# Half of a retention output projection as seven products on stored sums, and norms from a tile of ones

## The chip, the cores and the metric

The kernel runs on 1 core of one Trainium2 chip. The metric is the device time of one execution in microseconds (us), taken as the median of several runs. TensorE (PE in the profile) multiplies matrices, VectorE (DVE) and ScalarE (ACT) work element by element, GpSimd (POOL) and SyncE (SP) here mostly issue transfers (DMA) between the chip's DRAM and its on-chip memory. Every engine works through its own instructions in their written order; semaphores hold an instruction until what it needs is there.

## The reference, cut to what matters

The program is a two-layer encoder on 1024 tokens with 1024 features: forgetting attention, then a gated FFN, then retention, then a second gated FFN, with RMS norms between. The change lies in the retention layer:

```python
def retention(h, w_in, w_out):
    ...
    # per head (4 heads, value width 512), over chunks of 64 tokens:
    a = einsum(q, k) * d_intra;  inner = a @ v
    cross = (q @ state) * q_decay
    state = state * chunk_decay + (k * k_decay).T @ v
    y = inner + cross
    ...
    mu = jnp.mean(y, axis=-1, keepdims=True)
    var = jnp.mean(jnp.square(y - mu), axis=-1, keepdims=True)
    y = ((y - mu) * lax.rsqrt(var + EPS)).reshape(B, S, H * dv)
    return (jax.nn.silu(g) * y) @ w_out        # w_out: 2048 x 1024
```

So each head's output is normed for each token over 512 values, multiplied by its gate, and the four heads' 2048 features go through one projection to 1024.

## The kernel before

Features stand on the 128 partitions, tokens along the rows (two halves of 512). All products are made in float32 precision from two parts: `split` writes hi with ScalarE (a rounded copy) and lo = source - hi with VectorE, and a product is three matmuls, hi x hi, hi x lo and lo x hi. The instructions of each engine are put in order by a scheduler when the program is built; the pools (`bpa` with 32 buffers of 128x512, `bpb` with 24, `y`, `st` with 5 of 128x1024, `wp` for split weights) decide when a buffer may be written again.

The large projections, in the FFN among others, use seven products for a 2x2 block product in place of eight (`Products`, L672–L674): the operands are seven sums of the four blocks of each factor, named A11, S1, S2, A12, S3, A22, S4 on the side of the weights (made by `Blocks`) and B11, T1, T2, B21, T3, T4, B22 on the other (`Stored` or `Combos`). The output projection of the retention does not: it has 16 feature tiles and is done in two halves of 8, `mm_u` (L110–L112) with eight tiles of weights from `wtile2`. The first half adds the old residual (L1254), the second is `out_proj`.

The retention runs in eight stages (head h, token half ib). A stage makes the next stage's `scores` and weighs the values with its own (`weighted`, L1178–L1180; `crossed` with the state carried over, L1189–L1191), then calls `finish`, which evacuates the four outputs, sums their squares in `acc` (the mean has been taken off the values in `load_v`), and takes the norm: `colsum` (L165) multiplies the sums with a column of ones, so that tokens stand on partitions; `rsqrt` works on 128x4 values with ScalarE's square root; `rows` (L173) spreads the result over all partitions again. The tiles times this factor (for head 0 also times the gate g) are stored to `zd`. After the second half of a head, `prepare` loads the next head's k, q (`load_parts`, from `kd` and `qd`, in hi and lo parts) and v, and `state` makes its state. Behind the last stage `load_units` reads `zd` back, multiplies by the gates `gd` (for heads 1 to 3) and splits. All of these transfers stand in SP's one queue.

## Time and profile before

| | us |
|---|---|
| median of 3 runs | 2582.19 (2580.89 to 2583.51) |
| the profiled execution | 2582.71 |
| its span, first to last instruction | 2580.8 |
| PE, DVE, ACT, POOL busy in it | 2557.4, 1833.6, 1242.7, 210.1 |
| retention stages with their norms, about | 1583 to 1758 |
| first half of the output projection, about | 1758 to 1841 |
| second half, about | 1841 to 1927 |

A row of instructions gives the line, engine, operation, output <- inputs by the program's names and the shape, then busy time and mean length of one. A matmul's printed length overlaps the next one; what one costs is read from start to start. A wait is put down to what was released last.

### The profile page before, as it was taken

Reading aid. Unit: us, or ns where it says so; the run is one execution under the profiler, and the core shown is the slowest. Engines: PE = TensorE matmul, PEld = TensorE weight load, DVE = VectorE, ACT = ScalarE, POOL = GpSimd, SP = SyncE. Lnnn points to the kernel's source line nnn. Section 1 sums busy time; section 2 is a strip of 40 time slices with the busy share of each in tenths; the row PEclk is TensorE's granted clock in tenths of the full one; section 3 lists DMA queues with packets and bytes.
Section 4 is the critical chain, followed back from the end, with each engine's and each line's share of the span. In section 5 each row is a group of like instructions: output and inputs, shape, how many; then the busy total and the mean of one; then the engine's idle time right before and its main releaser. Section 6 shows DMA issues by size and latency. Waiting matters only on the chain.

```text
span 2580.8 us, 35315 instructions
## 1 busy us (share of the span) xinstructions
PE 2557.4 (99%) x12756; PEld 2177.7 (84%) x12756; DVE 1833.6 (71%) x3107; ACT 1242.7 (48%) x2331; POOL 210.1 (8%) x205
## 2 busy tenths in 40 slices
PE   9999999999999999999999999999999999999998
PEld 8889887888888887889898988988888888888888
DVE  6798888976666768886666576775668666668694
ACT  6566656643333455454444436552355333335543
POOL 0143323000000001001111110000000000000200
PEclk9999999999999999999999999999999999999999
DMA  3111142432332344533343335765522323225541
GB/s 131 45 58 59 57 147 85 157 110 95 114 106 94 124 162 155 182 112 115 121 141 123 127 135 191 254 220 191 205 101 87 106 98 110 101 84 192 169 150 66
DMA packets 148655, 327.86 MB, mean 127 GB/s; under 512 B 17280, under 2 KB 30592, under 8 KB 148480
## 3 DMA queue, kind: packets, MB, share of 16 engines
q1 hardware_dynamic: 143280, 310.38, 35.4%
q0 software_dynamic: 4480, 14.68, 1.7%
q8 instruction: 100, 1.64, 0.3%
q14 instruction: 75, 0.61, 0.1%
q10 hardware_dynamic: 720, 0.55, 0.1%
HBM read 225.40 MB, written 100.14 MB: 126 GB/s over the span
## 4 chain that ended last, share of the span: by engine, by line
PE 94%; DVE 2%; DMA 2%; issue 1%; ACT 1%; POOL 0%; SPq 0%; DVEq 0%; POOLq 0%; ACTq 0%
PE mm L672 18%; PE mm L673 18%; PE mm L674 18%; PE mm L110 7%; PE mm L111 7%; PE mm L112 7%; PE mm L792 2%; PE mm L790 2%; PE mm L791 2%; PE mm L279 1%; PE mm L278 1%; PE mm L277 1%; PE mm L1178 1%; PE mm L1180 1%; PE mm L1179 1%
## 5 line engine op out<-in xcount | busy, mean ns | idle before, releaser
L673 PE MATMUL mm<-b,wh 128*128 128x512 f32 x2128 | 827.9, 389 | 1.2 <-DVE b L103 1.2
L672 PE MATMUL mm<-b,wh 128*128 128x512 f32 x2128 | 825.7, 390 | 1.6 <-DVE 22_4485_22699 L732 0.8
L674 PE MATMUL mm<-b,wl 128*128 128x512 f32 x2128 | 824.3, 389 | 0.0
L102 ACT CAST wh<-st 128x512 fp32r<-128x512 f32 (+4 forms) x450 | 275.9, 615 | 496.1 <-PE mm L673 320.3
L672 PEld LDWEIGHTS mm<-b,wh 128*128 128x128 f32 x2128 | 399.5, 188 | 85.6 <-DVE 22_4485_22699 L732 1.2
L673 PEld LDWEIGHTS mm<-b,wh 128*128 128x128 f32 x2128 | 399.6, 188 | 83.6 <-DVE b L103 1.6
L674 PEld LDWEIGHTS mm<-b,wl 128*128 128x128 f32 x2128 | 399.5, 188 | 83.3 <-DVE wl L103 0.3
L103 DVE TENSOR_TENSOR wl<-st,wh 128x512 fp32r<-128x512 f32 (+4 forms) x450 | 310.6, 695 | 181.0 <-ACT wh L102 176.1
L102 ACT CAST wh<-s 128x512 fp32r<-128x512 f32 x252 | 156.4, 622 | 294.5 <-PE mm L673 256.0
L110 PE MATMUL mm<-b,wh 128*128 128x512 f32 x736 | 286.3, 393 | 7.2 <-ACT b L130 4.9
L111 PE MATMUL mm<-b,wh 128*128 128x512 f32 x736 | 287.4, 391 | 1.7 <-DVE b L103 1.7
L112 PE MATMUL mm<-b,wl 128*128 128x512 f32 x736 | 287.0, 391 | 0.0
L103 DVE TENSOR_TENSOR wl<-s,wh 128x512 fp32r<-128x512 f32 x252 | 180.3, 717 | 103.7 <-ACT wh L102 99.6
L110 PEld LDWEIGHTS mm<-b,wh 128*128 128x128 f32 x736 | 138.7, 188 | 36.6 <-ACT b L130 5.2
L111 PEld LDWEIGHTS mm<-b,wh 128*128 128x128 f32 x736 | 138.8, 189 | 29.5 <-DVE b L103 2.2
L112 PEld LDWEIGHTS mm<-b,wl 128*128 128x128 f32 x736 | 138.6, 188 | 28.6
L520 POOL DMA_DIRECT2D b<-ac_B x24 | 13.4, 559 | 1399.4 <-PE mm L673 1396.9
L791 PE MATMUL mm<-wl,b 128*128 128x256 f32 x448 | 126.4, 283 | 0.0
L790 PE MATMUL mm<-wh,b 128*128 128x256 f32 x448 | 126.2, 283 | 0.0
L792 PE MATMUL mm<-wh,b 128*128 128x256 f32 x448 | 126.0, 283 | 0.0
L624 DVE TENSOR_TENSOR s<-st 128x512 f32<-128x512 f32 x84 | 58.0, 691 | 74.3 <-DMA st<-ffn_in 35.3
L102 ACT CAST b<-st 128x512 fp32r<-128x512 f32 (+1 forms) x136 | 77.8, 606 | 53.3 <-DVE st L828 18.9
(527 smaller groups left out, 4118.8 us busy)
## 6 DMA issues: line engine op xcount, KB each, us to landing
st<-ffn_in SPq DMA_DIRECT2D x88, 512.0 KB, 3.6
st<-ffn_out_pairs SPq DMA_DIRECT2D x32, 512.0 KB, 4.1
ac_T<-t SPq DMA_DIRECT2D x48, 256.0 KB, 2.3
xo<-xd SPq DMA_DIRECT2D x32, 256.0 KB, 2.9
ac_B<-t SPq DMA_DIRECT2D x32, 256.0 KB, 2.4
st<-ac_T SPq DMA_DIRECT2D x16, 512.0 KB, 4.4
b<-ac_T POOLq DMA_DIRECT2D x32, 256.0 KB, 5.7
st<-ret_qk SPq DMA_DIRECT2D x16, 512.0 KB, 3.9
```

Of the source, the lines that this page charges most:

```text
L102: nc.scalar.copy(hi, src)
L103: return nc.vector.tensor_tensor(lo, src, hi.bitcast(F32), op=ALU.subtract)
L110: nc.tensor.matmul(ps, wh, xh, start=(first and k == 0), stop=False, skip_group_check=free)
L111: nc.tensor.matmul(ps, wh, xl, start=False, stop=False, skip_group_check=free)
L112: nc.tensor.matmul(ps, wl, xh, start=False, stop=(last and k == n - 1), skip_group_check=free)
L624: nc.vector.tensor_tensor(self.s1, self.a21, self.a22, op=ALU.add)
L672: nc.tensor.matmul(ps, hi[:, js], th, start=first and j == 0, stop=False, skip_group_check=True)
L673: nc.tensor.matmul(ps, hi[:, js], tl, start=False, stop=False, skip_group_check=True)
L674: nc.tensor.matmul(ps, lo[:, js], th, start=False, stop=(j == 3), skip_group_check=True)
L790: nc.tensor.matmul(o, th[:, tk], hi[:, js], start=f, stop=False, skip_group_check=True)
L791: nc.tensor.matmul(o, th[:, tk], lo[:, js], start=False, stop=False, skip_group_check=True)
L792: nc.tensor.matmul(o, tl[:, tk], hi[:, js], start=False, stop=(j == 3), skip_group_check=True)
```

## The change

1. **Seven products.** The feature tiles 0 to 7 (heads 0 and 1) of the output projection go through `Products` in four blocks of two output tiles. The weights' pieces are read from `ret_o` as 128x4x128 (`Blocks` with `rows`). The other side is a `Stored` object zc with the pools of MAP4. `finish` multiplies the gates in for heads 0 and 1, stores the first token half as B11 and B21, and after the second half reads these back (e0, o0), makes T1, T2, T3, T4 with four VectorE instructions per pair of tiles and stores them and B22. `zc.get` loads and splits them again by POOL's queue, during stages 5, 6 and 7. The tiles 8 to 15 are loaded by the new `Acts`, two at a time, during the last block of products.
2. **Norms.** `finish` splits `acc` and multiplies it with a 128x128 tile of ones (L1256, L1258), which gives the sum on every partition at once; a third matmul (L1257) adds the row of eps, scaled to fit, that lies in two rows of the tile ez and is loaded before each finish from `ed`. Ln and Exp on ScalarE and three VectorE instructions, all 512 wide, make the factor.
3. **One function table.** With Ln and Exp in place of the square root, one table is loaded ahead; kap, rho and the states are rescaled (`passed`) so that the sums of the norm keep in range.
4. **Queues.** The part loads of kd and qd are issued by POOL and not by SP.

The line numbers of the changed kernel are higher: L672–L674 become L693–L695, L103 becomes L106, L828 becomes L849. The orders below are the written orders of one engine, line, operation, output <- inputs, shape; names with numbers are buffers.

TensorE's work around the norm of one stage (head 1, first half) before the change, where cs and rw are the norm's two results among the matmuls of scores and state:

```order
L1152 MATMUL mm_16415<-b_16296,b_16254 128x384
L1153 MATMUL mm_16415<-b_16297,b_16254 128x384
L1154 MATMUL mm_16415<-b_16296,b_16255 128x384
L1152 MATMUL mm_16415<-b_16300,b_16258 128x384
L165 MATMUL cs_16221<-ones,yacc_16202 128x1 x4
L1153 MATMUL mm_16415<-b_16301,b_16258 128x384
L1154 MATMUL mm_16415<-b_16300,b_16259 128x384
```

and at the same norm now, with sm the sum, ah and al its split input:

```order
L1223 MATMUL mm_16401<-wh_16217,b_15871 128x256
L1256 MATMUL sm_16261<-ah_16257,ones 128x512
L1257 MATMUL sm_16261<-ez,ones 128x512
L1167 MATMUL mm_16615<-b_16352,b_16317 128x512
L1168 MATMUL mm_16615<-b_16353,b_16317 128x512
L1169 MATMUL mm_16615<-b_16352,b_16318 128x512
L1167 MATMUL mm_16615<-b_16358,b_16317 128x512
L1258 MATMUL sm_16261<-al_16258,ones 128x512
L1168 MATMUL mm_16615<-b_16359,b_16317 128x512
```

The column sums, and the later spread of rows with them, are replaced by three full-width matmuls, between other work as before.

VectorE in the finish of head 1's second half, now: fb is the norm's factor, g the gates, e and o (numbers 3224, 3225 and 3228, 3229) the first halves read back, t the sums:

```order
L1272 TENSOR_TENSOR yt_16536<-yt_16536,g_16570 128x512
L1272 TENSOR_TENSOR yt_16539<-yt_16539,g_16574 128x512
L1272 TENSOR_TENSOR yt_16544<-yt_16544,g_16578 128x512
L1272 TENSOR_TENSOR yt_16549<-yt_16549,g_16582 128x512
L1283 TENSOR_TENSOR t_3226_16587<-yt_16536,e_3224_16585 128x512
L1284 TENSOR_TENSOR t_3227_16588<-yt_16539,t_3226_16587 128x512
L1285 TENSOR_TENSOR yt_16536<-yt_16539,yt_16536 128x512
L1286 TENSOR_TENSOR o_3225_16586<-o_3225_16586,t_3227_16588 128x512
L1283 TENSOR_TENSOR t_3230_16602<-yt_16544,e_3228_16600 128x512
L1284 TENSOR_TENSOR t_3231_16603<-yt_16549,t_3230_16602 128x512
L1285 TENSOR_TENSOR yt_16544<-yt_16549,yt_16544 128x512
L1286 TENSOR_TENSOR o_3229_16601<-o_3229_16601,t_3231_16603 128x512
```

Before, only four multiplications by the factor stood here. Sixteen instructions are now in a row, ahead of the next norm's sums (yacc) and its split.

SP's queue at the same place, now, where zcB and zcT are the stored operands:

```order
L1282 DMA e_3224_16585<-zcB_15389 128x512
L1282 DMA o_3225_16586<-zcB_15393 128x512
L632 DMA st_17787<-ret_o 128x4x128
L1288 DMA zcB_15394<-yt_16539 128x512
L1288 DMA zcB_15394<-yt_16549 128x512
L1288 DMA zcT_15391<-t_3226_16587 128x512
L1282 DMA e_3228_16600<-zcB_15389 128x512
L1288 DMA zcT_15390<-t_3227_16588 128x512
L1288 DMA zcT_15392<-yt_16536 128x512
L1282 DMA o_3229_16601<-zcB_15393 128x512
L1288 DMA zcT_15395<-o_3225_16586 128x512
L1288 DMA zcT_15391<-t_3230_16602 128x512
```

The second pair's e (3228) is loaded behind the store of the first pair's t (3226), and its o (3229) behind two more stores.

The diff, without the lines that only rescale:

```diff
--- before.py
+++ after.py
...
@@ -527,6 +530,20 @@
     MAP2 = dict(zip(NAMES, (bpa, bpa, bpa, bpa, bpb, bpb, bpb)))
     MAP3 = dict(zip(NAMES, (bpa, bpa, bpa, bpb, bpb, bpb, bpa)))
 
+    MAP4 = dict(zip(NAMES, (bpa, bpa, bpb, bpb, bpb, bpa, bpa)))
+    ACTS = {"A11": (6, 7), "S1": (0, 1), "A12": (2, 3), "S3": (4, 5)}
+
+    class Acts:
+
+
+        def __init__(self, srcs):
+            self.srcs, self.t = srcs, {}
+
+        def get(self, i):
+            if i not in self.t:
+                self.t[i] = load_units(bpb if i < 6 else bpa, *self.srcs[i])
+            return self.t[i]
+
     class Combos:
         def __init__(self, gi, pools):
             self.gi, self.pools = gi, pools
@@ -605,12 +622,16 @@
     class Blocks:
 
 
-        def __init__(self, src):
+        def __init__(self, src, rows=False):
             self.s1, self.ready = None, {}
             sts = []
             for i in range(2):
                 st = sp.tile([P, 1024], F32, tag="st", name=nm("st"), bufs=5)
-                nc.sync.dma_start(st, src[:, i * 1024:(i + 1) * 1024])
+                if rows:
+                    for t in range(2):
+                        nc.sync.dma_start(st[:, HALF[t]].rearrange("p (j c) -> p j c", j=4), src[i][:, t])
+                else:
+                    nc.sync.dma_start(st, src[:, i * 1024:(i + 1) * 1024])
                 sts.append(st)
             self.a11, self.a12 = sts[0][:, 0:512], sts[0][:, 512:1024]
             self.a21, self.a22 = sts[1][:, 0:512], sts[1][:, 512:1024]
@@ -1056,11 +1077,30 @@
     nc.vector.tensor_tensor(r2, rc, rc, op=ALU.mult)
     kap = small([P, RET_HEADS, TB], "kap", 1)
     rho = small([P, RET_HEADS, TB], "rho", 1)
-    rho2 = small([P, RET_HEADS, TB], "rho2", 1)
+
...
+    ps = mp.tile([P, H], F32, tag="ms", name=nm("tr"))
+    n = RET_HEADS * TB
+    nc.tensor.transpose(ps[:n, :P], rho.rearrange("p h b -> p (h b)"), ident)
+    er = [yr("er")[:n, :P] for _ in range(2)]
+    nc.scalar.activation(er[0], ps[:n, :P], AF.Copy, scale=512 * EPS)
+    nc.vector.scalar_tensor_tensor(er[1], ps[:n, :P], 512 * EPS, er[0].bitcast(F32), op0=ALU.mult, op1=ALU.subtract)
+    ed = dp.tile([2, RET_HEADS * S], F32, tag="ed", name="ed")
+    for i, t in enumerate(er):
+        nc.gpsimd.dma_start(ed[i].rearrange("(n p) -> n p", p=P), t.bitcast(F32))
+    ez = sp.tile([P, H], F32R, tag="xo", name="ez", bufs=2)
+    nc.scalar.activation(ez, R[:, :H], AF.Copy, scale=0.0)
...
@@ -1081,7 +1121,7 @@
             for e in range(2):
                 r[e][i] = units(bpa)
                 for t, part in zip(r[e][i], src[e]):
-                    nc.sync.dma_start(t.bitcast(F32), part[:, HALF[i]])
+                    nc.gpsimd.dma_start(t.bitcast(F32), part[:, HALF[i]])
         return r
 
     def load_k(h):
@@ -1115,7 +1155,7 @@
             kt += [(hi[:, b * 256:(b + 1) * 256], lo[:, b * 256:(b + 1) * 256]) for b in range(2)]
         return ks, kt
 
-    def state(kt, vv):
+    def state(h, kt, vv):
 
         r = []
         for e in range(2):
@@ -1127,7 +1167,10 @@
                 nc.tensor.matmul(ps, kh[:, es], vh, start=(b == 0), stop=False)
                 nc.tensor.matmul(ps, kh[:, es], vl, start=False, stop=False)
                 nc.tensor.matmul(ps, kl[:, es], vh, start=False, stop=(b == 3))
-            r.append(bsplit(bpa, ps))
+            hi, lo = units(bpa)
+            nc.scalar.activation(hi, ps, AF.Copy, scale=passed[h])
+            nc.vector.scalar_tensor_tensor(lo, ps, passed[h], hi.bitcast(F32), op0=ALU.mult, op1=ALU.subtract)
+            r.append((hi, lo))
         return r
 
     zero = cp.tile([P, P], F32, tag="tri", name="zero")
@@ -1191,11 +1234,15 @@
                 nc.tensor.matmul(yps[vt], sl[:, vs], qh, start=False, stop=False)
 
     def finish(h, ib, yps):
+        nc.gpsimd.dma_start(ez.bitcast(F32)[:2, :], ed[:, h * S + ib * H:h * S + (ib + 1) * H])
         acc = sp.tile([P, H], F32, tag="sacc", name=nm("yacc"), bufs=2)
         ys = []
         for vt in range(4):
             y = yu("yt")
-            nc.scalar.copy(y, yps[vt])
+            cp_ = nc.scalar.copy(y, yps[vt])
+            if vt == h == ib == 0:
+                with tc.issue_after(cp_.ins):
+                    nc.scalar.preload_act_table_set("natural_log_exp_and_others")
             if vt == 0:
                 nc.scalar.activation(acc, y, AF.Square)
             else:
@@ -1203,24 +1250,47 @@
                 nc.scalar.activation(sq, y, AF.Square)
                 nc.vector.tensor_tensor(acc, acc, sq, op=ALU.add)
             ys.append(y)
-        cs = colsum(acc, mp, "ms")
-        var = small([P, 4], "yv")
-        rs = slice(4 * ib, 4 * ib + 4)
-        nc.vector.scalar_tensor_tensor(var, cs[:, 0:4], 1.0 / 512, rho2[:, h, rs], op0=ALU.mult, op1=ALU.mult)
-        r = rsqrt(var, 1.0, 4)
-        fac = small([P, 4], "yf")
-        nc.vector.tensor_tensor(fac, r, rho[:, h, rs], op=ALU.mult)
-        fb = rows(fac, mp, "ms")
+        hi, lo = yr("ah"), yr("al")
+        split(hi, lo, acc)
+        ps = mp.tile([P, H], F32, tag="ms", name=nm("sm"))
+        nc.tensor.matmul(ps, onesr, hi, start=True, stop=False)
+        nc.tensor.matmul(ps, onesr, ez, start=False, stop=False)
+        nc.tensor.matmul(ps, onesr, lo, start=False, stop=True)
+        q, fb = yu("q"), yu("fb")
+        nc.scalar.activation(q, ps, AF.Ln, scale=1.0 / 512)
+        nc.scalar.activation(q, q, AF.Exp, scale=-0.5)
+        nc.vector.scalar_tensor_tensor(fb, ps, -0.5 / 512, q, op0=ALU.mult, op1=ALU.mult)
+        nc.vector.tensor_tensor(fb, fb, q, op=ALU.mult)
+        nc.vector.scalar_tensor_tensor(fb, fb, 1.5, q, op0=ALU.add, op1=ALU.mult)
         for vt in range(4):
             nc.vector.tensor_tensor(ys[vt], ys[vt], fb, op=ALU.mult)
-            if h < 1:
-                g = yu("g")
-                nc.sync.dma_start(g, gd[4 * h + vt][:, HALF[ib]])
-                nc.vector.tensor_tensor(ys[vt], ys[vt], g, op=ALU.mult)
-            nc.sync.dma_start(zd[4 * h + vt][:, HALF[ib]], ys[vt])
-
+            if h > 1:
+                nc.sync.dma_start(zd[4 * h + vt][:, HALF[ib]], ys[vt])
+                continue
+            g = yu("g")
+            nc.sync.dma_start(g, gd[4 * h + vt][:, HALF[ib]])
+            nc.vector.tensor_tensor(ys[vt], ys[vt], g, op=ALU.mult)
+            if ib == 0:
+                j = 2 * h + vt // 2
+                nc.sync.dma_start(zc.d[("B11", "B21")[vt % 2]][:, j * H:(j + 1) * H], ys[vt])
+        if h < 2 and ib == 1:
+            for j in (2 * h, 2 * h + 1):
+                js = slice(j * H, (j + 1) * H)
+                e1, o1 = ys[j % 2 * 2:j % 2 * 2 + 2]
+                e0, o0, t1, t2 = yu("e0"), yu("o0"), yu("t1"), yu("t2")
+                for t, n in ((e0, "B11"), (o0, "B21")):
+                    nc.sync.dma_start(t, zc.d[n][:, js])
+                nc.vector.tensor_tensor(t1, e1, e0, op=ALU.subtract)
+                nc.vector.tensor_tensor(t2, o1, t1, op=ALU.subtract)
+                nc.vector.tensor_tensor(e1, o1, e1, op=ALU.subtract)
+                nc.vector.tensor_tensor(o0, o0, t2, op=ALU.subtract)
+                for n, t in (("T1", t1), ("B22", o1), ("T2", t2), ("T3", e1), ("T4", o0)):
+                    nc.sync.dma_start(zc.d[n][:, js], t)
+
+
+    zc = Stored("zc", MAP4, False)
     prepare(0)
-    heads[0][4] = state(heads[0][1], heads[0][3])
+    heads[0][4] = state(0, heads[0][1], heads[0][3])
     stages = [(h, ib) for h in range(RET_HEADS) for ib in range(2)]
     a = [scores(0, 0, dg) for dg in range(4)]
     for i, (h, ib) in enumerate(stages):
@@ -1230,6 +1300,9 @@
         yps = [mm_ps() for _ in range(4)]
         if ib == 1:
             crossed(h, yps)
+        if i == 7:
+            zc.get("T4")
+            zc.get("B22")
         an = []
         for dg in range(4):
             if nxt:
@@ -1238,21 +1311,40 @@
         a = an
         finish(h, ib, yps)
         if ib == 1 and nxt:
-            heads[h + 1][4] = state(heads[h + 1][1], heads[h + 1][3])
-
-    zg = list(zip(zd, [None] * (4 * 1) + gd[4 * 1:]))
+            heads[h + 1][4] = state(h + 1, heads[h + 1][1], heads[h + 1][3])
+        for n in {5: ("B11", "T1"), 6: ("T2", "B21"), 7: ("T3",)}.get(i, ()):
+            zc.get(n)
+
+
     y = [[None, None] for _ in range(KT)]
-    acts = [load_units(bpa, *t) for t in zg[:8]]
-    for n in range(KT):
-        w = wtile2(d["ret_o"][n], 8)
-        for h in range(2):
-            ps = mm_ps()
-            mm_u(ps, w, acts, h)
-            y[n][h] = yu("y")
-            xo = sp.tile([P, H], F32, tag="xo", name=nm("xo"), bufs=2)
-            nc.sync.dma_start(xo, xd2[n][:, HALF[h]])
-            nc.vector.tensor_tensor(y[n][h], ps, xo, op=ALU.add)
-    X, nrm, nw = out_proj(d["ret_o"], y, [load_units(bpb if i < 6 else bpa, *t) for i, t in enumerate(zg[8:])], xd, 3, d["ffn_in"][1, 0], MAP3)
+    acts = Acts(list(zip(zd[8:], gd[8:])))
+    banks[0] += 1
+
+    def blocks(n):
+        w = [d["ret_o"][2 * n + i][:, :D].rearrange("p (j t c) -> p t j c", t=2, c=P) for i in range(2)]
+        return Blocks(w, True)
+
+    prod = Products(blocks(0), zc).open()
+    for n in range(KT // 2):
+        u = {q: yu(q) for q in ("11", "12", "21", "22")}
+
+        def closed(b, c):
+            nc.scalar.copy(u["22"], b)
+            nc.vector.tensor_tensor(u["22"], c, u["22"], op=ALU.add)
+
+        prod.middle(lambda b: nc.scalar.copy(u["12"], b), closed)
+        nxt = Products(blocks(n + 1), zc, (acts, ACTS) if n == 2 else None).open() if n < 3 else None
+        prod.close()
+        nc.vector.tensor_tensor(u["12"], prod.c, u["12"], op=ALU.add)
+        for i in range(2):
+            for h in range(2):
+                t = u[f"{i + 1}{h + 1}"]
+                xo = sp.tile([P, H], F32, tag="xo", name=nm("xo"), bufs=2)
+                nc.sync.dma_start(xo, xd2[2 * n + i][:, HALF[h]])
+                nc.vector.tensor_tensor(t, ((prod.a, t), (prod.b, t))[i][h], xo, op=ALU.add)
+                y[2 * n + i][h] = t
+        prod = nxt
+    X, nrm, nw = out_proj(d["ret_o"], y, [acts.get(i) for i in range(8)], xd, 3, d["ffn_in"][1, 0], MAP3)
     ffn(1, X, nrm, xd, None, True, nw, MAP3)
 
 
```

More of the change, by code (lines that the diff above doesn't have):

```diff
@@ L78, in yu, with yr @@
         return yp.tile([P, H], F32, tag="y", name=nm(s))
+    def yr(s):
+        return yp.tile([P, H], F32R, tag="y", name=nm(s))
     def units(pool):
```

12 lines of the change are left out of this document (9 added, 3 removed).

## The prediction

> **What bounds the kernel now.** I read the page's busy shares first, then its chain of waits, then the stretch that the change touches, by windows.
>
> ```profile
> span 2580.8 us, 35315 instructions
> PE 2557.4 (99%) x12756; PEld 2177.7 (84%) x12756; DVE 1833.6 (71%) x3107; ACT 1242.7 (48%) x2331; POOL 210.1 (8%) x205
> PE 94%; DVE 2%; DMA 2%; issue 1%; ACT 1%; POOL 0%; SPq 0%; DVEq 0%; POOLq 0%; ACTq 0%
> ```
>
> TensorE (PE) is busy in 99% of the span and is 94% of the chain that ended last. So time is saved by taking TensorE instructions away, and lost where another engine then makes TensorE wait. The retention with its norms lies at about 1583–1758 us, the first half of the output projection at 1758–1841 us.
>
> ```profile
> 1600.00:1650.00 50.00, 49.27 (x277) 43.29 (x276) 37.60 (x86) 31.57 (x69) 0.00 (x0) 1.00 0.77 248
> 1650.00:1700.00 50.00, 50.00 (x316) 46.09 (x315) 37.84 (x96) 29.33 (x66) 0.00 (x0) 1.00 0.78 254
> 1700.00:1758.00 58.00, 57.51 (x329) 51.36 (x328) 42.03 (x93) 34.09 (x73) 0.00 (x0) 1.00 0.65 212
> ...
> PE mm L1178 <- ACT wh L1167: 0.7, 1, 0.7
> PE mm L1152 <- DMA b<-qd30h: 0.3, 1, 0.3
> ```
>
> The columns of the first rows are the stretch, its length, then the busy time of PE, PE's weight loads, DVE, ACT and POOL, the granted clock (1.00), the DMA share and GB/s. PE has no gap here; the waits (1583–1945 us) show its two longest, 1.0 us together. But DVE (VectorE) is busy for 117.5 of these 158 us, 74%, and the DMA engines for 65–78%. There is some room for new work there, and not much.
>
> **What the change takes from TensorE.** These rows give the pace of a 128x512 matmul and the two norm steps that go.
>
> ```profile
> 1629.70 0.39 PE L1178 MATMUL mm<-wh,b 128*128 128x512 f32 x1
> 1629.93 0.39 PE L1179 MATMUL mm<-wl,b 128*128 128x512 f32 x1
> 1630.16 0.95 PE L165 MATMUL cs<-ones,yacc 128*128 128x1 f32 x8
> 1630.97 0.49 PE L1180 MATMUL mm<-wh,b 128*128 128x512 f32 x1
> 1631.29 0.34 PE L1178 MATMUL mm<-wh,b 128*128 128x384 f32 x1
> 1631.47 0.33 PE L1179 MATMUL mm<-wl,b 128*128 128x384 f32 x1
> ...
> 1636.68 0.28 PE L1180 MATMUL mm<-wh,b 128*128 128x256 f32 x1
> 1636.80 1.05 PE L173 MATMUL rw<-ident,yf 128*128 128x128 f32 x8
> 1637.61 0.36 PE L1178 MATMUL mm<-wh,b 128*128 128x256 f32 x1
> 1637.81 0.28 PE L1179 MATMUL mm<-wl,b 128*128 128x256 f32 x1
> ...
> L173 PE MATMUL rw<-ident,yf 128*128 128x128 f32 x64 | 8.4, 274 | 0.0
> L165 PE MATMUL cs<-ones,yacc 128*128 128x1 f32 x64 | 7.6, 239 | 0.0
> ```
>
> From start to start, 128x512 costs 0.227 us, 128x384 0.18, 128x256 0.12. The printed 0.39 us overlaps the next and is not what one costs.
>
> 1. Products. Before, feature tiles 0–7 take 8 output tiles x 2 halves x 8 tiles x 3 matmuls = 384. After, 4 blocks x 7 products x 4 x 3 = 336, of the same shape. 48 x 0.227 = **-10.9 us**.
> 2. Norms. The column sums start at 1630.16 and the next matmul at 1630.97: 0.81 us, and that next one takes 0.32 instead of 0.227. The rows start at 1636.80 and end at 1637.61: 0.81, and the next takes 0.20 instead of 0.12. Together 1.79 us; the grouped rows have 64 records of each, 8 a finish, so eight finishes: **-14.3 us**.
> 3. In their place come 3 matmuls of 128x512 a finish: 24 x 0.227 = **+5.4 us**. One 128x128 transpose is added, costed as one of the four steps of L173 (0.81/4): **+0.2 us**.
>
> Sum on TensorE: **-19.6 us**. The profiled execution took 2582.71 us (its span and 1.9 us around it), 0.5 above the median of 2582.19, so with everything hidden the time would be 2563.1 us. The four function-table loads that go are ACT work beside a busy PE and count for nothing.
>
> **What comes back: VectorE.** What leaves TensorE lands on DVE: splits of the sums that come back from DRAM, five 512-wide steps and a split for each norm, the gates of head 1, 16 sums and differences. Its pace, again start to start:
>
> ```profile
> 1607.78 0.68 DVE L103 TENSOR_TENSOR b<-mm,b 128x512 fp32r<-128x512 f32 x1
> 1608.38 0.34 DVE L1163 SCALAR_TENSOR_TENSOR atd<-mm,kap,mask 128x128 f32<-128x128 f32 x1
> 1608.64 0.74 DVE L1074 SCALAR_TENSOR_TENSOR b<-st,vmean,b 128x512 fp32r<-128x512 f32 x1
> 1609.30 0.29 DVE L103 TENSOR_TENSOR wl<-atd,wh 128x128 fp32r<-128x128 f32 x1
> 1609.50 0.35 DVE L1163 SCALAR_TENSOR_TENSOR atd<-mm,kap,mask 128x128 f32<-128x128 f32 x1
> 1609.76 0.61 DVE L1168 SCALAR_TENSOR_TENSOR wl<-mm,kap,wh 128x384 fp32r<-128x384 f32 x1
> 1610.28 0.28 DVE L103 TENSOR_TENSOR wl<-atd,wh 128x128 fp32r<-128x128 f32 x1
> 1610.48 0.48 DVE L1168 SCALAR_TENSOR_TENSOR wl<-mm,kap,wh 128x256 fp32r<-128x256 f32 x1
> 1610.88 0.29 DVE L103 TENSOR_TENSOR wl<-atd,wh 128x128 fp32r<-128x128 f32 x1
> ```
>
> So 512 wide costs 0.60 us (0.66 with vmean), 384 wide 0.52, 256 wide 0.40, 128 wide 0.20 to 0.26. I counted the changed order on both engines between the same two events: the split that feeds the ones-matmul of the second finish (head 0, second half) and that of the last one (head 3, second half). DVE has 159 instructions 512 wide (11 with vmean), 4 of 384, 13 of 256 and 48 of 128: 95.4 + 0.7 + 2.1 + 5.2 + 11.0 = 114.4 us. PE has 320, 84 and 175 matmuls of 512, 384 and 256, and 16 transposes at 0.2: 72.6 + 15.1 + 21.0 + 3.2 = 111.9 us. In the last part, between the last two finishes, it is 19.9 us of DVE against 12.0 of PE, since the weight sums and splits of the first product blocks stand there. DVE has no slack left, and **2.5 us** are short even if it never stands still.
>
> It will stand still. DVE works in written order, and in finish the second pair's e0 is loaded only after the store of the first pair's t1 on the in-order SP queue (the orders of VectorE and of SP in the section on the change). From the end of t1, three more instructions (1.8 us) cover that load. Its landing time:
>
> ```profile
> zd<-yt SPq DMA_DIRECT2D x32, 256.0 KB, 2.9
> g<-gd SPq DMA_DIRECT2D x8, 256.0 KB, 4.9
> st<-gd SPq DMA_DIRECT2D x12, 512.0 KB, 4.7
> b<-ac_T POOLq DMA_DIRECT2D x32, 256.0 KB, 5.7
> ```
>
> A 256 KB transfer lands in 2.9 us (stores) to 4.9 us (loads of gates): 1.1 to 3.1 us uncovered, middle 2.1, once per head. Behind a standing DVE are the next scores' splits and the next acc sums, for which PE waits. Two heads: **4.2 us**. The stand-stills that DVE has today (below) I take as mostly filled by the longer queue; bounds of the whole DVE term 0 (its 74% today left TensorE only 1.0 us of waits) to 25 us (third rival), value **6.7 us**, nearer the low end because the count is of work and not of waits.
>
> **What comes back: transfers.** Operands now fill the pools until the last block, so all 16 loads of 512 KB for tiles 8–15 go through five st buffers in its time. Each tile holds two buffers for a landing (4.7 us), a 1024-wide multiply (twice 0.60) and two splits on ACT and DVE, some 8.5 us; two and a half tiles are in flight, so 3.4 us a tile and 27 us for eight. From the last finish to the projection's second half the written order has some 214 matmuls of 128x512, 48 us of cover; if the loads start late it is about half of that. Bounds 0 and 5 us, value **2 us**. The 48 loads of kd and qd move from SP to POOL: landing there is 5.7 us against 4.9 for SP's g, and the cover is most of a head's matmuls, so nothing; if that cover is gone, each of three heads pays the 0.8 us of difference.
>
> The nearest thing that the trace has to the new 28 reloads is the FFN's change of group, where as many are split within some 20 us:
>
> ```profile
> PE mm L673 <- DVE b L103: 1.2, 1, 1.2
> PE mm L672 <- DVE 22_1856_9302 L732: 0.8, 1, 0.8
> ...
> 989.82 1.90 POOL L520 DMA_DIRECT2D b<-ac_B  x3 [0.16 <-issue]
> ```
>
> There TensorE lost 2.0 us (975–1005 us). Here they are spread over three stages, which is why I add nothing for them beyond the DVE count.
>
> The Trainium skill, page "SBUF — State Buffer", section "SBUF: two separate sides", speaks against moving loads to POOL: transfers issued there need descriptors that GpSimd writes, and it is locked out while VectorE holds their shared ports in a two-port mode. The last row has three issues in 1.90 us, 0.63 each, beside a DVE that was splitting; no run here yet shows these loads beside a DVE with no gaps.
>
> **Sum:** 2582.7 - 19.6 + 6.7 + 2.0 = 2571.8, so **2572 us**.
>
> **Rivals.**
>
> *All hidden*, 2563 us: for it speaks today's 1.0 us of waits; against it the 114.4 us of DVE work beside 111.9. Chance 0.16.
>
> *The reloads of e0 and o0 in a crowd*, no change: with the DMA share at 0.78 already and some 8 MB more in the stretch (28 reloads, 8 reads of e0 and o0 and 12 more stores of 256 KB, less 8 loads of 512 KB), the landing doubles from 4.9 to 9.8 us; DVE then stands 9.8 - 1.8 = 8 us per head, 16 for both. 2582.7 - 19.6 + 2.5 + 16 + 2 = 2584 us. It decides from 4.7 us a head, where the sum passes 2577. Chance 0.22.
>
> *POOL issues wait out DVE*, no change: were each of the 16 part loads of a head held for one 0.60 us instruction, the last would be 9.6 us later; exposed at one head it makes 2582 us. The row of three issues in 1.90 us speaks against. The skill's rule above would be its cause. Chance 0.04.
>
> *DVE keeps its stand-stills*, slower. Its waits at 1583–1760 us:
>
> ```profile
> DVE yv L1209 <- PE cs L165: 9.6, 4, 4.8
> DVE b L1074 <- ACT b L1073: 9.4, 11, 1.7
> DVE wl L103 <- ACT wh L102: 4.9, 9, 2.1
> DVE b L103 <- ACT b L102: 4.7, 4, 2.0
> ```
>
> They make 28.6 us in 177, so 18 in 111.9. The same turn from TensorE to ScalarE to VectorE remains in each norm. With no slack, each of them is TensorE's wait: DVE costs 2.5 + 4.2 + 18 = 25 us, the time is 2582.7 - 19.6 + 25 + 2 = 2590 us. It decides once 15.6 of the 18 us remain, where the sum passes 2587.4. Against it: an engine with a full queue finds its inputs ready more often. Chance 0.18.
>
> That the products cost more than 0.227 us a matmul, so that the change saves less, I leave out: their form, a 128x128 weight tile against a moving 128x512, is that of the rows L1178 and L1179 above, and of what they replace.
>
> **Chances and range.** A measurement of this kernel tells about 0.2%, 5.2 us, from no change: faster is below 2577.0, slower above 2587.4. My forecast, with 2566–2577 as its own range, has 0.40; with all hidden, faster has 0.56. The crowd and POOL give 0.26 for the same, stand-stills 0.18 for slower. Below 2562 only a PE that also loses its old waits would come, above 2589 about half of the slow case: range 2562 to 2589.
>
> **What would show it.** In the changed profile: L693–L695 at 0.227 us; no L165 or L173 in the retention; PE idle of some 9 us in place of 1.0, most of it released by DVE between the sixth finish and the second product block; DVE over 90% busy there; DVE's t1 of the second pair waiting for a DMA by 1–3 us; the last block's waits for DMA or its splits below 5 us. I am wrong if PE's waits in the retention stay under 3 us (all hidden), or if DVE's waits for e0 exceed 7 us, for ACT 16 us, or for PE the share of them that L1209 has now.

## The result, and the profile after

| | before | changed |
|---|---|---|
| median, us | 2581.89 (5 runs, 2579.03 to 2583.51) | 2606.08 (5 runs, 2602.89 to 2611.77) |
| profiled execution, us | 2582.71 | 2603.95 |
| its span, us | 2580.8 | 2601.5 |

The changed kernel is slower: 1.0097 of the time before (95% interval 1.0083 to 1.0111). The forecast was 2572 us with a range of 2562 to 2589.

The page of the changed kernel, with the rows that answer to the first three of the prediction:

```profile
span 2601.5 us, 35255 instructions
PE 2552.2 (98%) x12605; PEld 2165.8 (83%) x12605; DVE 1884.7 (72%) x3161; ACT 1269.4 (49%) x2381; POOL 255.1 (10%) x291
PE 90%; DVE 3%; DMA 3%; issue 2%; ACT 1%; POOL 0%; SPq 0%; DVEq 0%; POOLq 0%
```

PE is busy for 5 us less, not 20, in a span that is 21 us longer, and its share of the chain fell from 94% to 90%. (The work of 19.6 us did go; the slow clock described below puts some 14 us of longer matmuls in its place.) The windows over the changed stretch (stretch, length, PE busy, PE's weight loads, DVE, ACT, POOL, granted clock, DMA share, GB/s) show two things:

```profile
1583.00:1640.00 57.00, 56.49 (x303) 48.94 (x302) 39.01 (x79) 38.47 (x77) 15.25 (x28) 1.00 0.70 225
1640.00:1700.00 60.00, 53.07 (x275) 46.17 (x274) 45.92 (x94) 28.75 (x65) 9.64 (x18) 0.94 0.80 275
1700.00:1760.00 60.00, 48.71 (x233) 41.12 (x232) 44.69 (x92) 30.77 (x69) 13.01 (x25) 0.86 0.65 222
1760.00:1800.00 40.00, 36.11 (x169) 30.34 (x168) 39.20 (x67) 28.40 (x54) 8.52 (x16) 0.96 0.63 211
1800.00:1850.00 50.00, 49.03 (x215) 40.01 (x215) 37.84 (x57) 19.94 (x35) 0.00 (x0) 1.00 0.59 207
1850.00:1900.00 50.00, 46.45 (x202) 37.49 (x201) 34.30 (x53) 21.41 (x37) 0.00 (x0) 1.00 0.61 206
```

First, PE stands: length less busy time is 27.1 us here, and 1.2 us in the same stretch before. Second, its clock was not always granted: one less the clock, times the length, is 3.6 + 8.4 + 1.6 = 13.6 us. With the prediction's sum for the work alone, 2563.1 + 25.9 + 13.6 = 2602.6 us, against 2603.95 of this execution. The prediction added 8.7 us for what comes back (6.7 for VectorE, 2.0 for the transfers of the last block); these two numbers make 39.5. The whole miss lies in them.

Where PE stood (its waits, sum, times and longest), and the matmuls behind the first long stop:

```profile
PE sm L1256 <- ACT ah L105: 10.2, 2, 5.3
PE mm L1232 <- ACT yt L1242: 4.0, 1, 4.0
PE mm L693 <- ACT yt L1242: 3.9, 1, 3.9
...
1679.53 0.79 PE L1256 MATMUL sm<-ah,ones 128*128 128x512 f32 x1 [5.32 <-ACT ah L105]
...
1680.55 0.63 PE L1167 MATMUL mm<-b,b 128*128 128x512 f32 x1
1680.98 0.63 PE L1168 MATMUL mm<-b,b 128*128 128x512 f32 x1
1681.40 0.63 PE L1169 MATMUL mm<-b,b 128*128 128x512 f32 x1
```

Four stops of 3.9 to 5.3 us carry 18 us. Behind the first, a 128x512 matmul takes 0.425 us from start to start in place of 0.227, for about 7 us. VectorE's own waits and the landings (KB each, us from issue to landing) say who was late:

```profile
DVE yt L1272 <- DMA g<-gd: 14.0, 5, 6.4
DVE t L1283 <- DMA e<-zcB: 7.5, 3, 3.3
...
g<-gd SPq DMA_DIRECT2D x16, 256.0 KB, 8.6
e<-zcB SPq DMA_DIRECT2D x4, 256.0 KB, 6.1
```

The second long stop, at head 1, shows the chain in the timeline (start, length, engine, instruction, in brackets the idle time before it and what ended it):

```profile
1703.43 5.12 SPq L632 DMA_DIRECT2D st<-ret_o  x7
1708.60 6.54 SPq L1271 DMA_DIRECT2D g<-gd  x4
...
1705.19 0.56 POOL L1124 DMA_DIRECT2D b<-qd30h  x1
...
1711.04 0.54 POOL L1124 DMA_DIRECT2D b<-qd31l  x1 [1.74 <-DMA b<-qd30h]
...
1720.18 2.69 DVE L1272 TENSOR_TENSOR yt<-yt,g 128x512 f32<-128x512 f32 x4 [6.37 <-DMA g<-gd]
...
1720.91 1.32 ACT L1242 COPY yt<-mm 128x512 f32<-128x512 f32 x2 [9.39 <-DVE yt L1272]
...
1721.54 0.79 PE L1232 MATMUL mm<-b,b 128*128 128x512 f32 x1 [4.04 <-ACT yt L1242]
```

SP's loads of weights and gates and POOL's loads of qd run at once. The gates are asked for late and land late: in the whole kernel SP's issue of one gate load takes up to 3.1 us (0.8 in E1 below, where POOL issues no part loads). VectorE stands 6.4 us; ScalarE's copy of the next outputs waits for tiles that VectorE holds, 9.4 us; and PE waits for the bank of its result memory that this copy empties.

The last of the four stops, ahead of the first block of products, is of another kind. VectorE is busy for 39.2 of the 40 us from 1760 us on, among the splits of the reloaded sums. ScalarE, in its own order, waits for reloads that have not landed, and the copy of the outputs that PE needs stands behind their splits:

```profile
ACT b L105 <- DMA b<-zcT: 5.2, 3, 2.8
...
1788.13 0.80 PE L693 MATMUL mm<-b,wh 128*128 128x512 f32 x1 [3.89 <-ACT yt L1242]
```

### The profile page after: what moved, and what is told of

It is laid out like the page before. It is cut to its first block, busy times and chain, and to the rows that moved or that the text cites. A ratio compares the mean times of both kernels' runs of the same rounds, so it can differ in the third digit from the quotient of the medians.

```text
span 2601.5 us, 35255 instructions
## 1 busy us (share of the span) xinstructions
PE 2552.2 (98%) x12605; PEld 2165.8 (83%) x12605; DVE 1884.7 (72%) x3161; ACT 1269.4 (49%) x2381; POOL 255.1 (10%) x291
## 4 chain that ended last, share of the span: by engine, by line
PE 90%; DVE 3%; DMA 3%; issue 2%; ACT 1%; POOL 0%; SPq 0%; DVEq 0%; POOLq 0%
PE mm L693 19%; PE mm L694 19%; PE mm L695 19%; PE mm L113 6%; PE mm L114 6%; PE mm L115 6%; PE mm L813 2%; PE mm L811 2%; PE mm L812 2%; PE mm L280 1%; PE mm L282 1%; PE mm L281 1%; DMA g<-gd 1%; DMA e<-zcB 1%; DMA st<-gd 1%
## 5 line engine op out<-in xcount | busy, mean ns | idle before, releaser
L693 PE MATMUL mm<-b,wh 128*128 128x512 f32 x2240 | 869.9, 390 | 7.7 <-ACT yt L1242 3.9
L695 PE MATMUL mm<-b,wl 128*128 128x512 f32 x2240 | 868.7, 389 | 0.0
L693 PEld LDWEIGHTS mm<-b,wh 128*128 128x128 f32 x2240 | 420.9, 188 | 97.5 <-ACT yt L1242 4.3
L695 PEld LDWEIGHTS mm<-b,wl 128*128 128x128 f32 x2240 | 420.9, 188 | 87.7
L106 DVE TENSOR_TENSOR wl<-st,wh 128x512 fp32r<-128x512 f32 (+4 forms) x450 | 310.8, 695 | 171.5 <-ACT wh L105 167.3
L105 ACT CAST wh<-s 128x512 fp32r<-128x512 f32 x264 | 163.8, 622 | 308.3 <-PE mm L694 271.8
L106 DVE TENSOR_TENSOR wl<-s,wh 128x512 fp32r<-128x512 f32 x264 | 188.5, 716 | 104.2 <-ACT wh L105 100.0
L114 PEld LDWEIGHTS mm<-b,wh 128*128 128x128 f32 x608 | 114.8, 189 | 24.6 <-DVE b L106 2.2
L115 PEld LDWEIGHTS mm<-b,wl 128*128 128x128 f32 x608 | 114.5, 188 | 23.4
L105 ACT CAST b<-st 128x512 fp32r<-128x512 f32 (+1 forms) x120 | 69.0, 605 | 49.8 <-DMA st<-ac_T 16.0
```

What stands on the lines that cost most here:

```text
L105: nc.scalar.copy(hi, src)
L106: return nc.vector.tensor_tensor(lo, src, hi.bitcast(F32), op=ALU.subtract)
L114: nc.tensor.matmul(ps, wh, xl, start=False, stop=False, skip_group_check=free)
L115: nc.tensor.matmul(ps, wl, xh, start=False, stop=(last and k == n - 1), skip_group_check=free)
L693: nc.tensor.matmul(ps, hi[:, js], th, start=first and j == 0, stop=False, skip_group_check=True)
L695: nc.tensor.matmul(ps, lo[:, js], th, start=False, stop=(j == 3), skip_group_check=True)
```

## The experiments

E1 is the base of several others, since it has one part less of the change. Each ratio is to the kernel before on the same chip, with its 95% interval.

**E1, the queue.** The part loads on SP again:

```diff
-                    nc.gpsimd.dma_start(t.bitcast(F32), part[:, HALF[i]])
+                    nc.sync.dma_start(t.bitcast(F32), part[:, HALF[i]])
```

> The changed kernel with the 48 part loads of kd and qd issued by SP again, as before; nothing else. In the changed kernel VectorE stood 14.0 us for gates that landed in 8.6 us (4.9 before) and TensorE had four stops of 4 to 5.3 us. Theory 'crowd by POOL': the part loads now run beside the gate loads and slow them; on SP the gates land in about 5 us again, VectorE's wait for them falls below 5 us, and the time falls by 10 to 25 us, to 2580-2596 us. Rival 'the gates and read-backs are late by their own place': behind 16 more loads in SP's order they come no earlier; 2600-2625 us.

2602.5 us, 1.0081 (1.0066 to 1.0096): 3.6 us less than the change, with runs that overlap (2601.1 to 2603.9 against 2602.9 to 2611.8). The gates landed in 5.7 us and VectorE no longer waited for them, as 'crowd' said, but the time did not follow; it lies in the range of the rival. The wait moved to the read-backs:

```profile
1710.57 0.69 DVE L1284 TENSOR_TENSOR t<-yt,t 128x512 f32<-128x512 f32 x1
...
1713.85 0.32 SPq L1282 DMA_DIRECT2D e<-zcB  x1
...
1721.09 0.69 DVE L1283 TENSOR_TENSOR t<-yt,e 128x512 f32<-128x512 f32 x1 [8.63 <-DMA e<-zcB]
...
1718.40 0.59 ACT L1242 COPY yt<-mm 128x512 f32<-128x512 f32 x1 [7.13 <-DMA zcB<-yt]
...
1726.61 0.80 PE L1256 MATMUL sm<-ah,ones 128*128 128x512 f32 x1 [5.82 <-ACT ah L105]
```

The first pair's t1 was ready when the next instruction started, at 1710.57. SP was still issuing qd parts and stores, and asked for the second pair's e at 1713.85; it landed 7.2 us later. VectorE stood 8.6 us, with the next norm's sums behind it in its order, and ScalarE stood 7.1 us for a tile whose store had not landed.

**E2, norms alone.** The kernel before with parts 2 and 3 of the change:

```diff
-        cs = colsum(acc, mp, "ms")
...
-        fb = rows(fac, mp, "ms")
+        split(hi, lo, acc)
+        nc.tensor.matmul(ps, onesr, hi, start=True, stop=False)
...
```

> The kernel before with the new norms alone (ones-matmuls, the row of eps, one function table, the rescaling); projection, gates and queues as before. By the prediction's sum this takes 14.3 us from TensorE and adds 5.4 + 0.2: 2582.2 - 8.7 = 2573 us. Theory 'late transfers' (the stops come from gates and read-backs, which this kernel does not have): 2570-2576 us, waits of TensorE below 3 us. Rival 'norm chain' (the longer way through Ln, Exp and three wide VectorE steps makes TensorE wait at the ones-matmul): two or more stops of some 5 us there, 2585-2600 us.

2572.2 us, 0.9963 (0.9949 to 0.9978), 9.2 us faster than before; the sum said 8.7. PE waited 1.0 us in the whole stretch. 'Norm chain' is out, and this version beats both kernels.

**E3, products alone.** Part 1 of the change, with the old norms and the part loads on SP.

> The kernel before with the seven products alone (gates of heads 0 and 1 and the sums in finish, stores, read-backs, reloads); norms and the part loads' queue as before. 48 matmuls less are 10.9 us. Theory 'late transfers': the stops and the slow clock behind them stay, 2595-2615 us. Rival 'VectorE work': without the 32 wide instructions of the new norms (19 us) VectorE has slack again and the time is 2571-2577 us; 'norm chain' gives the same 2571 us.

2593.0 us, 1.0044 (1.0029 to 1.0059), 2 us under the lower end for 'late transfers' and far from the 2571 to 2577 of the others. PE stood 16.0 us and lost 5.4 to the clock; VectorE waited 10.3 us for e. The products lose 11.6 us and the norms gain 9.2, which makes +2.4; together (E1) they lose 21.1. Nearly 19 us belong to neither part but to both.

**E4, no transfers.** The change without gate loads and read-backs, same instructions on VectorE:

```diff
-            g = yu("g")
-            nc.sync.dma_start(g, gd[4 * h + vt][:, HALF[ib]])
-            nc.vector.tensor_tensor(ys[vt], ys[vt], g, op=ALU.mult)
+            nc.vector.tensor_tensor(ys[vt], ys[vt], fb, op=ALU.mult)
...
-                nc.vector.tensor_tensor(t1, e1, e0, op=ALU.subtract)
+                nc.vector.tensor_tensor(t1, e1, fb, op=ALU.subtract)
```

> The changed kernel without the 16 gate loads and the 8 read-backs of e0 and o0: VectorE does the same instructions, with the norm's factor tile fb in the place of the gate and of the read-back tiles, so the retention's output is left without gates and the stored sums are of other numbers. Theory 'late transfers': all four stops go, and the time is that of the prediction's sum with its VectorE and last-block terms at most, 2562-2574 us, with no stretch at half clock. Rival 'VectorE work' (114.4 us of it beside 111.9 of TensorE): the work is unchanged, the stops stay, 2593-2606 us.

2585.1 us, 1.0013 (1.0003 to 1.0022): between the two theories. The transfers were worth 21 us, and 22 of loss remain. What remained was spread out:

```profile
1640.00:1700.00 60.00, 58.00 (x317) 51.00 (x316) 55.63 (x117) 34.95 (x79) 14.31 (x27) 0.97 0.72 237
1700.00:1760.00 60.00, 56.26 (x296) 49.27 (x294) 52.66 (x100) 38.39 (x80) 13.67 (x26) 0.97 0.65 224
```

DVE is busy for 55.6 and 52.7 of 60 us, where it had 45.9 and 44.7 with the transfers. The count of the prediction, a VectorE with hardly any slack, shows here; in the change itself it shows only from 1760 to 1800 us (39.2 of 40). A high share alone does not stop PE: in E2 VectorE is busy for 52.8 and 48.3 of these 60 us, and PE waited 1.0 us.

**E5, products without transfers.** E3 with the same left out.

> The kernel of the products alone, without its 16 gate loads and 8 read-backs; VectorE does the same instructions on resident tiles, so gates and old halves are left out of what is computed. The products alone took 2593.0 us: 2571.8 by the sum plus 14.8 us of new waits and half of 10.2 us at half clock. Theory 'read-backs': the two long stops behind VectorE's 10.3 us of waits for e go and with them the half clock; 2572-2577 us. Rival 'work and evacuations' (the stops come from ScalarE and VectorE having too much to do, as in the run of the whole change without transfers, 22 us over its sum): 2582-2590 us.

2589.3 us, 1.003 (1.0019 to 1.0041), 3.7 us less than E3; 'read-backs' had said 2572 to 2577, and the time is in the range of 'work and evacuations'. One stop of 3.4 us stayed at a norm, where ScalarE stood 7.5 us for a tile whose store as t1 had not landed, and one of 5.1 us appeared ahead of the projection's second half. My account of E3, that its stops were the read-backs, falls.

**E6, read-backs ahead.** E1 with both pairs' old halves loaded first, and q, fb, t1, t2 in other pools:

```diff
+                for n in ("B11", "B21"):
+                    old[j, n] = yu("e0")
+                    nc.sync.dma_start(old[j, n], zc.d[n][:, j * H:(j + 1) * H])
...
-        q, fb = yu("q"), yu("fb")
+        q, fb = qu("q"), qu("fb")
```

> The changed kernel with the part loads on SP (2602.5 us) in which both pairs' e0 and o0 are loaded ahead of the first pair's sums; for that q and fb move to the small pool of kf, and t1 and t2 to that of the scores' temporary. Computes the same. Theory 'order of the read-back' (the second pair's e is asked for behind the first pair's stores, so VectorE stands 8.6 us): that wait falls below 4 us, the stops of 3.5, 3.6 and 5.8 us at the norms shrink to 1-2 us, the half clock there (6.8 + 10.2 us) goes; 2580-2590 us. Rival 'the 16 buffers of y' or 'work': the loads wait for buffers in place of stores, 2597-2606 us.

2610.4 us, 1.0115 (1.0098 to 1.0132). VectorE waited less than 4 us for them, but PE now stood 11.6 us for a part load of qd and 7.2 us for a split; slower than either theory said.

**E7, no read-backs.** E1 with fb in the place of e0 and o0, as in E4.

> The changed kernel with the part loads on SP (2602.5 us) and without the read-backs (fb stands for e0 and o0, so the stored sums are of other numbers); gates are loaded. Theory 'read-backs': VectorE's 12.1 us of waits go, and of TensorE's 26.8 us of waits about 13, of the 27 us at half clock about 17, worth 8.5: 2578-2586 us. Rival 'work' (VectorE's 114 us beside 112): at most 8 us gained, 2594 us or more.

2596.6 us, 1.0056 (1.0041 to 1.0071): 5.9 us gained, less than half of what 'read-backs' said and in the range of 'work'. The 12 us of VectorE's wait went; ten stops of PE of 0.7 to 4.3 us were left, most of them behind splits and copies.

**E8, the norm's tiles elsewhere.** E1 with ah and al in the pool of split scores, q and fb in that of kf.

> The changed kernel with the part loads on SP (2602.5 us), where the norm's four new tiles leave the pool y of 16 buffers: ah and al go to the pool of the split scores, q and fb to the small pool of kf. Computes the same. Theory 'buffers of y' (a copy or a square on ScalarE waits until an old tile's store has landed, and the loads of gates and old halves until a tile is free): ScalarE's waits for stores and for VectorE at those copies fall, TensorE's 26.8 us of waits fall by 8 or more; 2582-2594 us. Rival 'work' (VectorE and ScalarE have no slack, whichever tile they wait for): 2598-2607 us. A third outcome, slower, would say that the other pools are as short.

2634.5 us, 1.0209 (1.0193 to 1.0224), the third outcome. SP's queue shows how a tile pool and a queue are tied together:

```profile
1639.64 2.13 SPq L1275 DMA_DIRECT2D zcB<-yt  x4
1642.11 1.64 SPq L1110 DMA_DIRECT2D st<-vd  x3
1643.80 1.37 SPq L1271 DMA_DIRECT2D g<-gd  x3
1645.27 0.63 SPq L1124 DMA_DIRECT2D b<-qd10h  x1
...
1651.00 1.54 PE L1195 MATMUL mm<-b,b 128*128 128x512 f32 x4 [12.77 <-DMA b<-qd10h]
```

The load of qd stood behind stores that waited for VectorE (one of them 10.4 us), and PE stood 12.8 us for it. Whether more buffers of y would help was not tried.

**E9 and E10, less work on VectorE.** E1 and E4, each without the 28 low splits of the reloaded sums:

```diff
+        if hi_only:
+            nc.scalar.copy(hi, lo.bitcast(F32))
+            return hi, hi
         split(hi, lo, lo.bitcast(F32))
```

> The changed kernel with the part loads on SP (2602.5 us), with 28 VectorE instructions left out: the reloaded sums are used as hi alone, so the products lack the low part of that operand (hi stands for it, and TensorE does as many matmuls). All transfers stay. Theory 'work': 28 x 0.60 = 16.8 us less of VectorE in the stretch from the sixth stage to the third product block, and TensorE's waits there go: 2584-2592 us. Theory 'transfers and buffers': the stops at the norms of head 1 and 2 are before most of that work and stay; 2596-2603 us.

> The same left out of the changed kernel without gate loads and read-backs (2585.1 us, 13.8 us of waits and 17 us at half clock over its sum of 2563.1). If transfers and VectorE's work are together the whole loss, this comes close to the sum: 2563-2570 us, waits below 5 us. Rival 'a third cause' (the order in which ScalarE evacuates, the tensor banks): 2576-2585 us.

E9: 2597.5 us, 1.0066 (1.005 to 1.0083), 5.0 less than E1 and in the range of 'transfers and buffers'. The stops around the norms stayed (12.6 us in three, 12.9 in E1). The work taken off VectorE did remove the stop ahead of the first block of products (6.0 us in E1), but one of 7.3 us now stood ahead of the projection's second half. E10: 2583.3 us, 1.0007 (0.9998 to 1.0017), 1.8 less than E4, which is within the spread of the runs; so the rival 'a third cause', though neither of the two that I had named for it. Its waits name another:

```profile
PE mm L113 <- ACT wh L105: 6.5, 1, 6.5
...
1782.54 0.35 SPq L850 DMA_DIRECT2D st<-zd  x1
...
1825.44 0.32 SPq L853 DMA_DIRECT2D st<-gd  x1
```

In the product blocks the waits nearly went, so PE came to the second half sooner and stood 6.5 us for its weights: SP issues those behind the 16 loads of tiles 8–15, which took from 1782.5 to 1825.4 us through the five st buffers.

**E11, filled stops, at the wrong place.** E1 with work that nobody uses:

```diff
+        if h < 2 and ib == 1:
+            for _ in range(6):
+                nc.tensor.matmul(ps, ones, ys[3], start=True, stop=True)
```

> The changed kernel with the part loads on SP (2602.5 us), with six matmuls that nobody uses (ones times the last evacuated tile, plain float32, about 0.9 us each) ahead of the ones-matmuls of the second halves of heads 0 and 1, where TensorE stood for 3.5 and 5.8 us. Computes the same. Theory 'a stop of TensorE costs its length and then half the clock for 3.4 to 10 us': with the stops filled the half clock behind them (6.8 and 10.2 us) shrinks to 0 to 7 us, while VectorE and ScalarE are as late as before: 2594-2600 us, though TensorE does 10.8 us of work more. Rival 'the half clock has another cause': it stays, and the filling costs what it exceeds the stops by, 2602-2607 us.

2604.3 us, 1.0091 (1.0076 to 1.0106). The stops are at the norms of the first halves of heads 1 and 2; I had put the filling one stage too early (it ran from 1645.5 us on, the last of it at 1700.5), so the stop of 5.8 us was still there and nothing is told of the clock. It does show that 10.6 us more work for PE cost only 1.8 us, within the spread of the runs.

**E12, half of the late loads.** E10 without the eight gate loads and multiplications of the last block.

> The run without gate loads, read-backs and low splits (2583.3 us) without the eight gate loads of 512 KB and the eight 1024-wide multiplications of the last block as well, so that heads 2 and 3 lack their gates too. There TensorE stood 6.5 us ahead of the projection's second half with 6.8 us at half clock behind it, and 16 loads took from 1782 to 1831 us. Theory 'the five st buffers in the last block': with eight loads that stop goes, with its half clock: 2571-2575 us, within 10 us of the sum of 2563.1. Rival 'the weights of the second half are late for another reason': 2580-2584 us.

2575.6 us, 0.9981 (0.9971 to 0.999): the stop of 6.5 us is gone, as 'five st buffers' said, and the time is 0.6 us over its range. Loads and multiplications went together here, so the run does not tell which of them held the five buffers.

**E13, filled at the norm.** E11 with the right condition:

```diff
+        if h in (1, 2) and ib == 0:
```

> As the run with filled stops, but with the six unused matmuls (ones times the last evacuated tile, plain float32, 0.89 us each as measured there) at the norms of the first halves of heads 1 and 2, directly ahead of the ones-matmul at which TensorE stood 3.5 and 5.8 us in the run with the part loads on SP (2602.5 us; 14.1 us lost to the granted clock). Computes the same. Theory 'a stop halves the clock': the stops at those two norms go to below 1.5 us and the half clock behind them shortens from 6.8 and 10.2 us to at most 3.4 each (the second has a stop of 3.6 us ahead of it); the loss to the clock falls from 14.1 to 6-10 us, and with 10.6 us of work in 9.3 us of stops the time is 2595-2601 us. Rival 'the half clock has another cause': as long as before, 14 us lost, 2602-2605 us.

2594.5 us, 1.0049 (1.0034 to 1.0064): 8 us faster than E1, with 10.6 us more work for TensorE.

```profile
1640.00:1700.00 60.00, 60.00 (x325) 51.52 (x325) 53.47 (x111) 35.32 (x75) 1.50 (x3) 1.00 0.88 296
1700.00:1760.00 60.00, 54.84 (x271) 44.73 (x270) 47.39 (x93) 32.86 (x72) 10.31 (x20) 0.97 0.71 245
...
1725.89 0.51 PE L1259 MATMUL sm<-ah,ones 128*128 128x512 f32 x1 [0.72 <-ACT ah L105]
```

In E1 these two windows had a clock of 0.94 and 0.91, and over the whole stretch 14.1 us were lost to it; here 5.4, a little less than the 6 to 10 of the theory, as the time is just under its range. A stop of 3.9 us was left ahead of the second filling. That the half clock follows TensorE's stops, and is a cost of its own, is shown by this run.

**E14, the queue without late transfers.** E2 with the part loads on POOL.

> The norms alone (2572.2 us, TensorE waiting 1.0 us) with the part loads of kd and qd moved to POOL as in the change. Theory 'a queue matters only where something waits in it': no transfer is late in that kernel, so the same time, 2570-2574 us. Rival 'POOL's transfers land later or hold VectorE up': 2575-2582 us, with waits of TensorE or VectorE for kd or qd.

2573.2 us, 0.9962 (0.9948 to 0.9977), the same as E2. The rival was right about the landings all the same: the gates landed in 7.6 us (5.5 in E2) and the first part loads of kd in 7.0 to 8.4 (4.9 to 5.9 in E2), and VectorE stood 1.5 us for gates. PE waited 1.0 us, as in E2. So the move to POOL makes transfers later by itself, and costs no time where there is slack for it.

**All of them by one account.** TensorE's work by the prediction's sum, its waits from 1583 to 1960 us over the 1.2 of before, and what the clock took there (from windows like those above), against the profiled execution:

| kernel | work | waits | clock | sum | measured |
|---|---|---|---|---|---|
| the change | 2563.1 | 25.9 | 13.6 | 2602.6 | 2604.0 |
| E1 | 2563.1 | 25.5 | 14.1 | 2602.7 | 2601.1 |
| E2 | 2574.0 | -0.2 | 0.0 | 2573.8 | 2572.2 |
| E3 | 2571.8 | 14.8 | 5.4 | 2592.0 | 2592.1 |
| E4 | 2563.1 | 12.6 | 8.8 | 2584.5 | 2585.1 |
| E5 | 2571.8 | 10.4 | 7.1 | 2589.3 | 2587.6 |
| E7 | 2563.1 | 19.4 | 11.5 | 2594.0 | 2597.7 |
| E9 | 2563.1 | 23.4 | 15.2 | 2601.7 | 2597.1 |
| E10 | 2563.1 | 12.5 | 7.1 | 2582.7 | 2584.2 |
| E11 | 2573.7 | 21.3 | 12.3 | 2607.3 | 2606.3 |
| E12 | 2563.1 | 7.0 | 1.2 | 2571.3 | 2574.9 |
| E13 | 2573.7 | 14.8 | 5.4 | 2593.9 | 2594.7 |
| E14 | 2574.0 | -0.2 | 0.0 | 2573.8 | 2573.2 |

Where stops are longest a stop inside a slow stretch is counted twice: E9 comes out 5 us too high, and E6 and E8, left out of the table, 7 and 13.

## Why the prediction was wrong

**What TensorE is spared: right.** The norms alone gave 9.2 us for 8.7, and with the prediction's savings as the work, all rows of the table but E9 come out to within 4 us.

**VectorE has no slack: right as a count, and the wrong thing to price.** The 114.4 us of work beside 111.9 show in E4, at 88 to 93% busy. In the change DVE was busy for only 74 to 77% of 1640–1760 us, since it stood for transfers; I had expected over 90%, which came only at 1760–1800 us. The failed step is "The stand-stills that DVE has today (below) I take as mostly filled by the longer queue", with a value of 6.7 us nearer the low end. What the runs showed in its place: VectorE stood 21.5 us for gates and read-backs, PE's waits grew by 25.9 us, the slow clock added 13.6, and without those transfers (E4) the time fell by 21.0. A full queue does not fill a stand-still when it works in order: in E1 the next norm's sums queued 8.6 us behind one read-back. By the prediction's own signs, too, the waits for e (7.5 us) exceeded the 7 that it set.

**The gates: not charged.** Gates counted as eight more multiplications, and their loads at nothing. VectorE stood 14.0 us for them, as they landed in 8.6 us beside POOL's loads. With those back on SP they landed in 5.7 and the wait went to the read-backs, so the queue chose who was late, and the time changed by only 3.6 us. The step that priced the move to POOL at nothing took each transfer by itself: "landing there is 5.7 us against 4.9". In the change the first part loads of kd landed in 7 to 9 us. The rule weighed there (the Trainium skill, page "SBUF — State Buffer", section "SBUF: two separate sides") showed no price in time: E14 is E2 to within 1 us, with POOL issuing beside VectorE. That the landings grew there is no proof of it; no run tells that rule from mere crowding.

**The read-backs: right place, wrong size.** 4.2 us were charged, 7.5 measured in the change and 12.1 in E1. I let SP ask for e as soon as t1 was done; it asked 3.3 us later, being busy with other transfers, and the landing took 7.2 us where I took up to 4.9. Uncovered are 3.3 + 7.2 - 1.9 = 8.6 us at head 1, not 2.1. And what stands behind a standing VectorE was named too narrowly: not only its next splits and sums, but ScalarE's copies, which need tiles that VectorE or an unlanded store still holds, and so the banks that PE writes to.

**The reloads: not charged.** "I add nothing for them beyond the DVE count" missed ScalarE, which waited 5.2 us for reloads, beside a VectorE that was full, and let PE stand 3.9 us in the change and 6.0 in E1. E9, with 28 VectorE instructions fewer, lacks this stop.

**The last block: right as a place, sized for one case.** 2 us were charged; in the change PE stood about 3.5 us from 1850 us on, and 6.5 us in E10, where it came earlier. The loads took 42 and 43 us from the first issue to the last, where "27 us for eight" tiles was the estimate. A saving upstream is paid back here: E12 shows it for E10, and E9 and E5 have stops of 7.3 and 5.1 us at the same place.

**The clock: missing.** Every wait was priced at its length. 13.6 us, half of what the waits themselves cost, came on top. The trace of before had shown this price, at 394 us, outside the stretch that the prediction reads:

```profile
394.93 0.50 PE L111 MATMUL mm<-b,wh 128*128 128x512 f32 x1 [1.74 <-DVE b L103]
...
396.20 0.63 PE L349 MATMUL st<-qh,kh 128*128 128x512 f32 x1
396.63 0.63 PE L350 MATMUL st<-ql,kh 128*128 128x512 f32 x1
...
395.00:400.00 5.00, 5.00 (x18) 4.13 (x18) 2.97 (x6) 2.21 (x4) 2.42 (x3) 0.66 0.34 107
```

Behind a short stop the pace is 0.43 us a matmul and the window's clock 0.66. The length alone does not decide: this stop stands in all 16 profiled executions (1.7 to 1.9 us), and half clock follows it in five of them (before, the change, E8, E9 and E14). The Trainium skill, page "TensorE: Matmul & The Clock Gate", section "Part 1: The HAM clock gate (the "warmup" mystery)", says that the array falls to half clock after an idle window of about 3.4 us and comes back after a busy one; the trace agrees with the halving (0.425 us for 0.227) and in that 28 of 29 stops of 3.4 us or more brought it (counted over all 16 profiles at 1583–1960 us; the exception is one of 3.6 us at 1715 us in E1). It does not agree in that ten of 15 between 2.2 and 3.4 us, and here even one of 1.7, brought it too.

**The rivals.** Of the four, 'DVE keeps its stand-stills' had the sign, and its 2590 us lacked the gates and the clock. That its 25 us for VectorE are close to the 25.9 that PE waited is luck: the long waits were for transfers, and VectorE's waits for ScalarE, from which most of it was worked out, are 24.6 us in E2 as well (1583–1760 us), where PE waited only 1.0 us. 'The reloads in a crowd' had the mechanism, landings that nearly double (4.9 to 8.6 us for g), and priced it as no change because it counted the read-backs alone. Both were held to be alternatives; they came together, and with the last block behind them.

What stays open: without transfers, low splits and late gates (E12) the kernel is still 12.5 us over its sum, and 3.4 us slower than the norms alone; 8.2 of it are the waits and the clock that its profile shows, spread over stops of at most 1.7 us. Why the two parts lose 19 us more together than apart is argued from the shared tiles and from VectorE's full queue, and not shown; the two runs that moved tiles to other pools (E6, E8) only moved the wait.

## What to carry to other kernels

Where the bound engine has no gaps today, price a wait at its length and then at the slow clock that may follow it, here half as much again in sum; read that second price in any stop that the old trace has. When work is moved onto an in-order engine that will be full, list every transfer that it consumes there, with the landing it has in the crowd that the change itself makes, and with the place in the queue that asks for it. Time two halves of a change apart: here one half alone gained 9.2 us, while the whole lost 24.2.
